# Two attention layers on one core: ones column in layer B's values, the gate folded into the last output weights, activations in two tiles

## The chip, the cores and the metric

The program runs on one core of a Trainium2 chip, with its matrix engine (PE), three elementwise engines (DVE, ACT, POOL) and a queue engine (SP) that issues nearly all transfers. The metric is the device time of one execution in microseconds, the median of several runs.

## What is computed

Two layers over 1024 tokens of width 1024, with 256 context tokens beside them, one batch. Layer A is grouped-query attention with 16 query and 4 key heads, and layer B is neighbourhood attention (a window of 8 rows by 16 columns on a 16 x 64 grid, and all context tokens) with a learned bias. In both, a gate path `silu(z)` multiplies the attention's output ahead of the output projection.

```python
def reference(x, c, ctx, c_ctx, norm_g, w_mod, b_mod, ...):
    for i in range(DEPTH):                      # 0: gqa_axial_mixer, 1: neighbourhood_mixer
        sh_x, sc_x, g_x = jnp.split((silu_c @ w_mod[i] + b_mod[i])[:, None, :], 3, axis=-1)
        hx = rms_norm(x, norm_g[i]) * (1.0 + sc_x) + sh_x
        hc = rms_norm(ctx, norm_g[i]) * (1.0 + sc_c) + sh_c
        ...
        x = x + g_x * yx
    return rms_norm(x, final_norm_g)

# in neighbourhood_mixer, for one row of the grid
s_nb = einsum('bqhd,bqkhd->bhqk', qr, kw) * ATTN_SCALE + bias
s_cx = einsum('bqhd,bshd->bhqs', qr, kc) * ATTN_SCALE
p = softmax(concatenate([s_nb, s_cx], -1))
o = p[..., :n_nb] @ vw + p[..., n_nb:] @ vc
yx = (o * silu(z)) @ w_out
```

## The kernel before

**Numbers.** Every float32 factor is held as a high and a low float16 part, and a product is three matmuls: high x high, high x low, low x high. So each tile is "split" (a cast, then a subtraction), weights are scaled by `WS` = 32, and each weight, activation and probability tile exists twice.

**Stages.** Layer A takes the span up to about 700 us. Then comes its output projection (`a_out`, one call for each 128-token tile and each half of the columns), interleaved with layer B's normalisation: `ln_pair` normalises two token tiles xa, xb (four blocks of 512 values a1, a2, b1, b2), forms the combinations that a Strassen-Winograd product needs, splits them and has the DMA transpose them into `hx`. `hx` holds seven blocks for each pair of token tiles: blocks 0 to 2 come from the "a" transposes (`hrb0a`, `hrb2a`, `hrb4a`, `hrb6a`, L701), blocks 3 to 6 from the "s" transposes (`hrb0s` ... `hrb6s`, L712). The string `"l0 o4 l2 o5 o6 l4 o7 o80 l6 o90"` sets the order of these steps.

Layer B works in eight pairs of heads, u = 0 to 7. `b_load` loads and combines a pair's weights, `b_qk` and `b_vz` project it (`winograd`: seven products, tiles `pwq..` and `pwv..`, and the context's products `pbc`, `pvc`), and `b_att` does its attention: scores into `bsn` and `bsc`, the bias added with a running maximum on DVE (L1613), exponentials on ACT as float16 (`bph`) and float32 (`bpf`) with their sums as a second output (L1631 to L1634), the low part by a subtraction on POOL or DVE (`p_split`: each `BEV`-th call goes to DVE whole, the others to POOL in two halves), a DMA transpose, and the product with the values (L1642, L1644) into `bpv`. `fin` divides by the sums, multiplies by the gate path and hands the result to `o_out`, which splits and transposes it into `ob[u]`.

The final projection is cut into two parts over the eight pairs. `b_part` multiplies pairs 0 to 5 for one token tile and one half of the columns, and `b_out` does pairs 6 and 7 of both halves, then the final norm and the store. Each `b_part` ends with a multiply by the gate row `g1` (DVE, L1751) and an add to the residual tile `acc` (POOL, L1752; DVE for the last tile). `ob` of pairs 0 to 6 goes through DRAM (`ob_d`) and comes back as `obf` in the memory of `hx`.

**Order.** The code records generators with due times: an item `(generator, start, end, total)` of `timeline` spreads its steps over that stretch of "pairs", so `b_att(u)` runs from u to u + 1 beside `b_proj(u + 1)`. The class `Planner` then takes all recorded instructions, simulates the five engines with its own costs, and writes an order for each engine; five rounds of `refine` reorder by due times, and the best is kept. So an edit in one place can change the order everywhere, layer A included.

## Time and profile before

| | |
|---|---|
| median of three runs | 1360.35 us (1357.03 to 1361.37) |
| the profiled execution | 1362.21 us, of which the span of instructions is 1360.3 |
| mean granted PE clock | 0.991 |
| PE matmuls | 1309.5 us busy, 14492 instructions |
| DVE, ACT, POOL busy | 1129.6, 976.2, 909.9 us |
| HBM read, written | 91.03 MB, 15.75 MB |

A matmul's record lasts longer than the time to the next start, since matmuls overlap in the pipeline; what a stream of them costs is read from start to start. The view of stretches gives the busy time of each engine in chosen windows and the granted PE clock. The view of groups gives all instructions of one line, tile and shape with the total and mean. A row `x3` of the timeline is three instructions that follow each other.

### The profile page before, as it was taken

How to read it: one execution, taken by the hardware profiler on the slowest of the kernel's cores; microseconds unless marked ns; L12 is line 12 of the kernel's file. 1: busy time of each engine (PE TensorE's matmuls, PEld its weight loads, DVE VectorE, ACT ScalarE, POOL GpSimd, SP SyncE). 2: the span in 40 equal slices, each digit the busy share in tenths (PEclk: the TensorE clock that was granted, in tenths of full speed). 3: DMA queues.
4: the chain of work that ended last, by engine and by line, in shares of the span. 5: the costliest groups of instructions: out<-in, count | busy, mean ns of one | idle time of the engine just before them, and what ended most of it. 6: DMA issues, size and time to landing. Idle time of an engine off the chain costs nothing.

```text
span 1360.3 us, 37879 instructions
## 1 busy us (share of the span) xinstructions
PE 1309.5 (96%) x14492; PEld 923.2 (68%) x14492; DVE 1129.6 (83%) x2603; ACT 976.2 (72%) x2325; POOL 909.9 (67%) x1251
## 2 busy tenths in 40 slices
PE   8999999999999999999999899999999999999994
PEld 4467777777777777776654357868677686876551
DVE  5898687978898787769448898899999999999668
ACT  4654889888888777788733355897978889787443
POOL 2323778777777767788775566586676778755565
PEclk9999999999999999999999999999999999999997
DMA  9634566787874222245237953587677768679953
GB/s 368 186 114 114 118 125 144 153 153 146 141 142 104 66 77 60 57 118 139 79 109 175 219 109 90 115 151 146 121 142 151 150 130 173 126 165 257 262 113 124
DMA packets 390350, 191.58 MB, mean 141 GB/s; under 512 B 349776, under 2 KB 355088, under 8 KB 390168
## 3 DMA queue, kind: packets, MB, share of 16 engines
q1 hardware_dynamic: 389592, 189.13, 61.6%
q8 instruction: 113, 1.85, 0.6%
q14 instruction: 69, 0.57, 0.1%
q10 hardware_dynamic: 576, 0.03, 0.0%
HBM read 91.03 MB, written 15.75 MB: 78 GB/s over the span
## 4 chain that ended last, share of the span: by engine, by line
PE 49%; DVE 24%; ACT 11%; issue 6%; DMA 5%; POOL 4%; DVEq 0%; POOLq 0%; SPq 0%; ACTq 0%
PE pa L1034 12%; PE pob L1747 5%; PE st L1260 3%; PE st L1261 3%; DVE wb L1435 3%; PE pm L1068 3%; PE poa L1353 2%; PE pv L1137 2%; PE pv L1136 2%; PE pv L1138 2%; DVE bpf L1613 2%; DVE bk L1504 2%; DVE bmx L1620 2%; ACT bpf L1633 1%; ACT bph L1631 1%
## 5 line engine op out<-in xcount | busy, mean ns | idle before, releaser
L1130 POOL TENSOR_TENSOR pl<-pf,ph 128x256 f16<-128x256 f32 x400 | 274.8, 712 | 83.3 <-ACT pf L1247 59.0
L1130 POOL TENSOR_TENSOR bph<-bpf,bph 128x256 f16<-128x256 f32 (+1 forms) x192 | 167.5, 889 | 119.0 <-ACT bpf L1633 98.7
L1034 PE MATMUL pa<-wa,x 128*128 128x256 f16 x1536 | 219.3, 272 | 1.0 <-DVE q L822 1.0
L1245 ACT ACTIVATE ph<-st 128x512 f16<-128x512 f32 x240 | 143.2, 602 | 56.4 <-PE st L1261 55.1
L1560 PEld LDWEIGHTS <-hx 128*128 128x128 f16 x2688 | 156.7, 98 | 11.7 <-issue 4.9
L1034 PEld LDWEIGHTS <-x 128*128 128x128 f16 x1536 | 139.7, 97 | 33.2 <-DVE q L822 1.3
L1247 ACT ACTIVATE pf<-st 128x512 f32<-128x512 f32 x240 | 143.2, 603 | 1.9 <-POOL pl L1130 1.2
L1069 DVE TENSOR_REDUCE mxp<-pm 128x1 f32<-128x512 f32 x192 | 127.5, 683 | 16.2 <-PE pm L1068 15.1
L1137 PE MATMUL pv<-v,ph 128*128 128x64 f16 x960 | 122.5, 195 | 0.0
L1136 PE MATMUL pv<-v,ph 128*128 128x65 f16 x960 | 122.1, 193 | 0.0
L1138 PE MATMUL pv<-v,pl 128*128 128x65 f16 x960 | 121.5, 192 | 0.4 <-POOL pl L1130 0.4
L1512 PEld LDWEIGHTS <-wb 128*128 128x128 f16 x672 | 63.5, 99 | 81.2 <-issue 10.9
L1130 POOL TENSOR_TENSOR qpp<-qpf,qpp 128x256 f16<-128x256 f32 (+1 forms) x158 | 94.2, 621 | 33.8 <-ACT qpf L1203 25.7
L1631 ACT ACTIVATE bph<-bpf,bnx 128x384 f16<-128x384 f32 (+1 forms) x128 | 69.9, 581 | 55.7 <-DVE bnx L1623 35.6
L1136 PEld LDWEIGHTS <-ph 128*128 128x128 f16 x960 | 90.7, 96 | 23.2 <-DVE og L1118 1.7
L1137 PEld LDWEIGHTS <-ph 128*128 128x128 f16 x960 | 90.3, 97 | 14.4 <-issue 0.4
L1138 PEld LDWEIGHTS <-pl 128*128 128x128 f16 x960 | 91.1, 99 | 9.4 <-POOL pl L1130 1.1
L1260 PE MATMUL st<-q,k 128*128 128x512 f16 x240 | 90.9, 379 | 1.9 <-ACT pf L1247 1.2
L1261 PE MATMUL st<-q,k 65*128 65x512 f16 x240 | 91.2, 381 | 0.0
L1353 PE MATMUL poa<-woa,oa 128*128 128x512 f16 x384 | 89.7, 379 | 0.0
L1747 PE MATMUL pob<-wob,obf 128*128 128x512 f16 x336 | 79.9, 379 | 0.2 <-DVE tmb L1751 0.2
L1633 ACT ACTIVATE bpf<-bpf,bnx 128x384 f32<-128x384 f32 (+1 forms) x128 | 74.4, 581 | 0.2
(486 smaller groups left out, 4045.6 us busy)
## 6 DMA issues: line engine op xcount, KB each, us to landing
wg<-in_w_mb SPq DMA_DIRECT2D x32, 512.0 KB
wsb<-in_b_wp SPq DMA_DIRECT2D x64, 256.0 KB
wm<-in_w_m SPq DMA_DIRECT2D x16, 512.0 KB
wsa<-in_a_wq SPq DMA_DIRECT2D x32, 256.0 KB
xstage<-in_x SPq DMA_DIRECT2D x8, 512.0 KB
wsoa<-in_a_w_out SPq DMA_DIRECT2D x16, 256.0 KB
x<-in_x SPq DMA_DIRECT2D x8, 512.0 KB
x_d<-x SPq DMA_DIRECT2D x8, 512.0 KB
```

Source lines behind the costliest of these rows:

```text
L1034: T.matmul(ps[:, :, i, :], hA(a, kt, t), wt[w][:, kt, :], start=n == 0, stop=n == 3 * KT - 1)
L1069: V.tensor_reduce(mxs[i][:, t, ch:ch + 1], pm, axis=AX.X, op=ALU.max)
L1130: G.tensor_tensor(lo[:, c], p32[:, c], hi[:, c], op=ALU.subtract)
L1136: T.matmul(pv[:, t, :], hi[:, c], v[:, 0:65], start=first and t == 0, stop=False)
L1137: T.matmul(pv[:, t, 0:HD], hi[:, c], v[:, 65:129], start=False, stop=False)
L1138: T.matmul(pv[:, t, :], lo[:, c], v[:, 0:65], start=False, stop=last and t == n - 1)
L1245: S.activation(ph, st, AF.Exp)
L1247: S.activation(p32, st, AF.Exp)
L1260: T.matmul(so, k1[:, g, kc], q1[:, :, i, :], start=True, stop=False)
L1261: T.matmul(so, k2[0:65, g, kc], q2[0:65, :, i, :], start=False, stop=True)
L1560: T.matmul(ps[:, t * P:(t + 1) * P], hx[a][:, t, blk, kt], wt[j][:, s_, w, kt], start=first and t == 0 and m == 0, stop=last and t == 3 an ...
L1747: T.matmul(ps, ob[kt][:, t, a], wout["b"][hf][b][:, kt, :], start=n == 0, stop=n == 3 * len(kts) - 1)
```

## The change

- **Values.** The value tile gets a column that holds 2 WS^2 (`v1_` is 130 wide: 64 high, the column, 64 low). The product with the probabilities becomes three matmuls of 65, 64 and 65 columns, as in layer A, and the sum of the probabilities arises in PSUM. The sums on ACT, their reduction, and the old `fin` go; `o_evict`, layer A's, takes its place. `BEV` becomes 8.
- **Gate.** `load_wout` multiplies the last output weights by the gate row (POOL) before the split. `b_part` ends with one add on DVE.
- **Activations.** `hx` becomes two tiles for each float16 part, one for blocks 0 to 2 and one for blocks 3 to 6. The final projection's `obf` (two tiles of three pairs) and `acc` (two of four token tiles) take their memory. Pair 6 is no longer stored and reloaded.
- **Residuals** are loaded by halves where `b_part` begins. Final norm: the first half is scaled on ACT and multiplied on POOL, except for the last tile.
- **Smaller ones.** `ln_pair` exchanges DVE and POOL in its combinations, and `a_out` adds tile 7 on DVE. `b_load` does its combinations in three POOL operations, one of them 256 wide. The second copy of q is made by ACT from the source. `b_att(7)` is due by 7.6, the weights from 6.6, `b_out` from 7.61.

```diff
-BEV, BLAG = 4, 4
+BEV, BLAG = 8, 4
...
-            DM.dma_start_transpose(d[:, t, 0:3].rearrange("p a k q -> p (a k) q"),
+            DM.dma_start_transpose(d[0][:, t].rearrange("p a k q -> p (a k) q"),
                                    s_[:, 0:3].rearrange("p a c -> p (a c)"))
         yield 900
-        G.tensor_tensor(b2, b1, b2, op=ALU.add)
-        V.tensor_tensor(b1, a1, b1, op=ALU.subtract)
-        G.tensor_tensor(a1, b2, a1, op=ALU.subtract)
+        V.scalar_tensor_tensor(b2, b1, -1.0, b2, op0=ALU.mult, op1=ALU.subtract)
+        G.tensor_tensor(b1, a1, b1, op=ALU.subtract)
+        V.scalar_tensor_tensor(a1, b2, -1.0, a1, op0=ALU.mult, op1=ALU.subtract)
         V.tensor_tensor(a2, a2, a1, op=ALU.subtract)
...
+                gw = bl.tile([P, 512], F32, name=f"gw{hf}", tag="gw", bufs=1)
+                DM.dma_start(gw, gate[:, hf * 512:(hf + 1) * 512].broadcast_to([P, 512]))
...
+                        G.tensor_tensor(st, st, gw, op=ALU.mult)
...
-            G.tensor_tensor(x1[:, hc], x1[:, hc], tm, op=ALU.add)
+            (V if t == NX - 1 else G).tensor_tensor(x1[:, hc], x1[:, hc], tm, op=ALU.add)
...
-    hx = [bpool.tile([P, 4, 7, 4, P], F16, name=f"hx{p}", tag=f"H{p}") for p in range(2)]
+    hx = [[bpool.tile([P, 4, 3 + j, 4, P], F16, name=f"hx{p}{j}", tag=f"H{p}{j}") for j in range(2)] for p in range(2)]
...
-            G.tensor_tensor(t1, b12, b11, op=ALU.subtract)
-            G.tensor_tensor(t2, b22, t1, op=ALU.subtract)
-            G.tensor_tensor(t3, b22, b12, op=ALU.subtract)
+            G.tensor_tensor(tt[:, 0:2], st[:, 1:3], b12.unsqueeze(1).broadcast_to([P, 2, P]), op=ALU.subtract)
+            G.tensor_tensor(t2, b22, t1, op=ALU.add)
...
-        v1_ = bq.tile([P, NT, 2, P], F16, name=f"bv1{u}", tag="v1")
+        v1_ = bq.tile([P, NT, 2, 130], F16, name=f"bv1{u}", tag="v1")
+        G.memset(v1_[:, :, :, HD:HD + 1], 2.0 * WS * WS)
...
-                    V.tensor_copy(ov[0][oth, i, ts], ov[0][own, i, ts])
+                    S.activation(ov[0][oth, i, ts], src, AF.Copy, scale=sc)
...
-                        S.activation(pf[:, 0:n], pf[:, 0:n], AF.Exp, bias=m, accum_out=sums[:, t % 4, 0:1])
-                        S.activation(pf[:, n:n + 2], cx_, AF.Exp, bias=m, accum_out=sums[:, t % 4, 1:2])
+                        S.activation(pf[:, 0:n], pf[:, 0:n], AF.Exp, bias=m)
+                        S.activation(pf[:, n:n + 2], cx_, AF.Exp, bias=m)
...
-                                T.matmul(pv[:, t % 4, :], pht[:, x_], v1_[:, kt, i, :], start=t % 4 == 0 and x_ == 0,
-                                         stop=False)
-                                T.matmul(pv[:, t % 4, 0:HD], plt[:, x_], v1_[:, kt, i, 0:HD], start=False,
+                                T.matmul(pv[:, t % 4, 0:65], pht[:, x_], v1_[:, kt, i, 0:65],
+                                         start=t % 4 == 0 and x_ == 0, stop=False)
+                                T.matmul(pv[:, t % 4, 0:HD], pht[:, x_], v1_[:, kt, i, 65:129], start=False, stop=False)
+                                T.matmul(pv[:, t % 4, 0:65], plt[:, x_], v1_[:, kt, i, 0:65], start=False,
                                          stop=t % 4 == 3 and x_ == len(keys) - 1)
...
+                    o_evict(bl, pv, og, 4, sz, hf * 4, i, f"b{u}{i}{hf}")
...
-        items.append((b_att(u), u, u + 1, C_BA))
+        items.append((b_att(u), u, u + (1 if u + 1 < NPAIR else 0.6), C_BA))
...
-        obf = bpool.tile([P, NPAIR - 1, NX, 2, P], F16, name="obf", tag="H0")
+            obf = bpool.tile([P, 3, NX, 2, P], F16, name=f"obf{p}", tag=f"H{p}0")
...
+        if not kts[0]:
+            DM.dma_start(fin_c["acc"][t][:, hcs], x1_d[t * P:(t + 1) * P, hcs])
...
-        tm = bq.tile([P, 512], F32, name=f"tmb{t}{hf}{kts[0]}", tag="cc")
-        V.tensor_tensor(tm, ps, fin_c["g1"][:, hcs], op=ALU.mult)
-        eng.tensor_tensor(fin_c["acc"][t][:, hcs], fin_c["acc"][t][:, hcs], tm, op=ALU.add)
+        V.tensor_tensor(fin_c["acc"][t][:, hcs], ps, fin_c["acc"][t][:, hcs], op=ALU.add)
...
+            if hf or t == NX - 1:
+                V.scalar_tensor_tensor(x2[:, hcs], x2[:, hcs], rs[:, 0:1], fg[:, hcs], op0=ALU.mult, op1=ALU.mult)
+            else:
+                S.activation(x2[:, hcs], x2[:, hcs], AF.Copy, scale=rs[:, 0:1])
+                G.tensor_tensor(x2[:, hcs], x2[:, hcs], fg[:, hcs], op=ALU.mult)
```

What the planner made of it is shown at two places; line numbers of the change differ by a few from those of before.

First, DVE at the end of layer B's normalisation, of before. `x16` and `x17` are token tiles 6 and 7, `L677` and `L678` normalise them, `L690` writes the low part that the transposes `hrb6a` and `hrb6s` take, and `L705`, `L707` form combinations:

```order
L658 TENSOR_SCALAR ms_ln_14266<-lssb6b_14264 128x1
L677 SCALAR_TENSOR_TENSOR x16_14056<-x16_14056,rs_ln_14258,lrow10_13846 128x512
L690 TENSOR_TENSOR hrb4s1_14150<-x14_13892,hrb4s0_14149 128x512
L678 TENSOR_TENSOR x16_14056<-x16_14056,lrow00_13844 128x512
L677 SCALAR_TENSOR_TENSOR x17_14161<-x17_14161,rs_ln_14268,lrow10_13846 128x512 x2
L678 TENSOR_TENSOR x17_14161<-x17_14161,lrow00_13844 128x512 x2
L677 SCALAR_TENSOR_TENSOR x16_14056<-x16_14056,rs_ln_14258,lrow10_13846 128x512
L690 TENSOR_TENSOR hrb6a1_14253<-x17_14161,hrb6a0_14252 128x512
L678 TENSOR_TENSOR x16_14056<-x16_14056,lrow00_13844 128x512
L690 TENSOR_TENSOR hrb6a1_14253<-x16_14056,hrb6a0_14252 128x512
L705 TENSOR_TENSOR x17_14161<-x16_14056,x17_14161 128x512
L690 TENSOR_TENSOR hrb6a1_14253<-x16_14056,hrb6a0_14252 128x512
```

The same place in the change, up to the last split of `hrb6s`:

```order
L690 TENSOR_TENSOR hrb6a1_14255<-x16_14058,hrb6a0_14254 128x512
L690 TENSOR_TENSOR hrb6a1_14255<-x17_14163,hrb6a0_14254 128x512
L690 TENSOR_TENSOR hrb6a1_14255<-x16_14058,hrb6a0_14254 128x512
L704 SCALAR_TENSOR_TENSOR x17_14163<-x17_14163 128x512
L1366 TENSOR_TENSOR tm80_14251<-poa80_14226,gt8_14222 128x512
L1443 SCALAR_TENSOR_TENSOR wb000_14358<-wsb000_14360,wb000_14358 128x3x128
L706 SCALAR_TENSOR_TENSOR x16_14058<-x17_14163,x16_14058 128x512
L690 TENSOR_TENSOR hrb6s1_14289<-x17_14163,hrb6s0_14288 128x512
L707 TENSOR_TENSOR x16_14058<-x16_14058 128x512
L690 TENSOR_TENSOR hrb6s1_14289<-x17_14163,hrb6s0_14288 128x512
L690 TENSOR_TENSOR hrb6s1_14289<-x16_14058,hrb6s0_14288 128x512 x2
```

The three splits of `hrb6a` stand together, and the combination between them (`L705`, which took POOL's `L704`) has left for POOL; `L704` and `L706` came from POOL to DVE.

The queue SP at that place, of before (`lrow` are the context's scale and shift rows, `wsb` a weight tile):

```order
L712 DMA_TRANSPOSE hx1_13800<-hrb4s1_14150 128x16x128
L671 DMA lrow11_14448<-mod_d_100 128x1024
L671 DMA lrow01_14446<-mod_d_100 128x1024
L701 DMA_TRANSPOSE hx0_13799<-hrb6a0_14252 128x12x128
L701 DMA_TRANSPOSE hx1_13800<-hrb6a1_14253 128x12x128
L1426 DMA wsb010_14643<-in_b_wp 128x512
L712 DMA_TRANSPOSE hx0_13799<-hrb6s0_14286 128x16x128
```

And of the change:

```order
L712 DMA_TRANSPOSE hx11_13802<-hrb4s1_14152 128x16x128
L701 DMA_TRANSPOSE hx00_13799<-hrb6a0_14254 128x12x128
L701 DMA_TRANSPOSE hx10_13801<-hrb6a1_14255 128x12x128
L1435 DMA wsb010_14642<-in_b_wp 128x512
L671 DMA lrow11_14447<-mod_d_100 128x1024
L671 DMA lrow01_14445<-mod_d_100 128x1024
L712 DMA_TRANSPOSE hx01_13800<-hrb6s0_14288 128x16x128
```

The two `lrow` loads moved from ahead of the `hrb6a` transposes to behind them.

Second, POOL at the end of the program, of before (`acc` with `tmb` is the residual add of a half tile, `rs_fin` the power of the final norm):

```order
L1752 TENSOR_TENSOR acc_23352<-acc_23352,tmb506_24463 128x512
L1752 TENSOR_TENSOR acc_23352<-acc_23352,tmb516_24475 128x512
L660 TENSOR_TENSOR rs_fin_24343<-ms_fin_24341,mhalf_75 128x1
L660 TENSOR_TENSOR rs_fin_24378<-ms_fin_24376,mhalf_75 128x1
L1752 TENSOR_TENSOR acc_23352<-acc_23352,tmb606_24498 128x512
L1752 TENSOR_TENSOR acc_23352<-acc_23352,tmb616_24510 128x512
L660 TENSOR_TENSOR rs_fin_24413<-ms_fin_24411,mhalf_75 128x1
```

And of the change (`fg` is the final norm's weight row):

```order
L660 TENSOR_TENSOR rs_fin_24796<-ms_fin_24794,mhalf_75 128x1
L1763 TENSOR_TENSOR acc1_23715<-acc1_23715,fg_23716 128x512
L660 TENSOR_TENSOR rs_fin_24828<-ms_fin_24826,mhalf_75 128x1
L660 TENSOR_TENSOR rs_fin_24860<-ms_fin_24858,mhalf_75 128x1
L1763 TENSOR_TENSOR acc1_23715<-acc1_23715,fg_23716 128x512 x2
L660 TENSOR_TENSOR rs_fin_24892<-ms_fin_24890,mhalf_75 128x1
```

The residual adds have left POOL. The multiplies by `fg` of tiles 4 to 6 stand among the powers, and two of them ahead of the last power, which is tile 7's.

87 lines of the change are left out of this document (38 added, 49 removed).

## The prediction

> **What bounds the kernel now.** I read the busy table first, then the stretches by stage, then the waits, and only then single instructions.
>
> ```profile
> PE 1309.5 (96%) x14492; PEld 923.2 (68%) x14492; DVE 1129.6 (83%) x2603; ACT 976.2 (72%) x2325; POOL 909.9 (67%) x1251
> ```
>
> TensorE is busy for 96% of the span of 1360.3 us. Whatever is to be won lies in the other 51 us, and whatever adds matmuls is paid in full. Where those 51 us lie is told by the view of stretches (columns: stretch, its length, then busy time and instructions of PE, PEld, DVE, ACT and POOL, then the granted PE clock, the DMA share and GB/s).
>
> ```profile
> 102.00:748.00 646.00, 637.63 (x7689) 462.21 (x7687) 499.12 (x1212) 488.28 (x1061) 470.49 (x677) 1.00 0.53 117
> 748.00:816.00 68.00, 61.17 (x387) 32.17 (x386) 63.04 (x91) 30.79 (x57) 42.27 (x49) 0.92 0.74 165
> 816.00:1326.00 510.00, 498.98 (x5723) 369.66 (x5721) 458.06 (x1043) 391.29 (x1067) 348.54 (x470) 1.00 0.73 153
> 1326.00:1361.00 35.00, 16.14 (x75) 6.94 (x72) 28.36 (x51) 10.71 (x29) 20.31 (x20) 0.77 0.32 120
> ```
>
> PE is idle for 8.4 us in layer A, which the diff hardly touches. It is idle for 6.8 us in the change of layers (748 to 816), where its clock also falls to 0.92 on average, a further loss of 68 x 0.08 = 5.4 us. Eight pairs of layer B leave 11.0 us idle, and the end, to 1360.3, leaves 18.2 us; what is missing from 51 lies in the first 102 us. The change works on the last three stretches shown.
>
> **The end.** The timeline gives the last matmuls and the chain behind them.
>
> ```profile
> 1341.91 0.81 PE L1747 MATMUL pob<-wob,ob 128*128 128x512 f16 x3
> ```
> ```profile
> 1350.35 0.68 DVE L1752 TENSOR_TENSOR acc<-acc,tmb 128x512 f32<-128x512 f32 x1
> 1350.45 0.63 ACT L1760 ACTIVATE jk<-acc 128x512 f32<-128x512 f32 x1 [1.53 <-DVE ms_fin L658]
> ```
> ```profile
> 1354.12 0.15 DVE L1761 TENSOR_TENSOR fss<-fss,fss 128x1 f32<-128x1 f32 x1
> 1354.31 0.15 DVE L658 TENSOR_SCALAR ms_fin<-fss 128x1 f32<-128x1 f32 x1
> 1354.61 0.55 POOL L660 TENSOR_TENSOR rs_fin<-ms_fin,mhalf 128x1 f32<-128x1 f32 x1 [2.66 <-DVE ms_fin L658]
> 1355.19 1.42 DVE L1765 SCALAR_TENSOR_TENSOR acc<-acc,rs_fin,fg 128x512 f32<-128x512 f32 x2 [0.73 <-POOL rs_fin L660]
> ```
>
> The last matmul ends at 1342.7 and the span at 1360.3: 17.6 us without matmuls. They go to a backlog of multiply (DVE), add (POOL) and normalise (DVE) for each half tile; the last residual add starts only 7.6 us after the last matmul. With the gate in the weights, an eviction is one add. My new chain: 0.2 from PE to DVE, the add 0.68, the square 0.63 and its read 0.19, the two small DVE steps 0.30, the power 0.55, two normalises 1.42, some 0.7 for the links, and from their end (1356.6) to the span's end 3.7 as now: 8.4 us. The POOL rows of the change put tile 6's multiply ahead of the last power, and that multiply waits for ACT's scaling of tile 6, which stands behind the last square. I add 1.6 for it (ACT's scaling and one POOL operation of 1.4, the row L1752 below, less the DVE steps that they overlap): 10.0. Gain 7.6; 0.6 us of PE gaps since 1326 (16.7 less 16.1 busy) could go too, but for each tile DVE will have about 2.5 us of work (two adds, a normalise and small steps) beside 2.6 us of matmuls (12, at 0.22 from start to start), and a normalise that meets POOL lasts longer. I take **-7**, with bounds -9 and -4.
>
> **The third matmul.** For every key block and query tile the change turns two matmuls (128 and 64 columns) into three (65, 64, 65). Layer A has this form already, so both are in the trace.
>
> ```profile
> L1642 PE MATMUL bpv<-bv,bpht 128*128 128x128 f16 x608 | 68.7, 220 | 1.1 <-DMA bpht<-bph 1.0
> ```
> ```profile
> 900.78 0.22 PE L1642 MATMUL bpv<-bv,bpht 128*128 128x128 f16 x1
> ...
> 901.12 0.38 PE L1512 MATMUL pwq2b<-hx,wb 128*128 128x512 f16 x1
> ```
> ```profile
> 560.99 0.19 PE L1136 MATMUL pv<-v,ph 128*128 128x65 f16 x1
> 561.01 0.20 PE L1137 MATMUL pv<-v,ph 128*128 128x64 f16 x1
> ...
> 561.42 0.38 PE L1261 MATMUL st<-q,k 65*128 65x512 f16 x1
> ```
>
> Durations overlap, so only starts count. From 900.78 to 901.12 stand four key blocks in the old form: 85 ns each. From 560.99 to 561.42 stand 14 matmuls of the new form: 31 ns each, 92 ns for three. 608 x 7 ns = **+4.3**, bounds +3 and +6, all on the path.
>
> The Trainium skill, "TensorE: Matmul & The Clock Gate", section "Back-to-back issue gap", speaks against this edit: a real stream of weight load and matmul is said to sustain about 81 ns per matmul at 128 columns. By that rule 608 more would cost 49 us; the starts above, 31 ns apart, disagree with it.
>
> **Relief of the helpers in layer B.** The waits of PE in 816 to 1326 are short and mostly for DVE. The longest:
>
> ```profile
> PE pwv7c L1560 <- DVE bv L1542: 1.3, 1, 1.3
> ```
>
> DVE is 90% busy there (458 of 510). What the change takes from it and from ACT, by the groups:
>
> ```profile
> L1659 DVE TENSOR_TENSOR boc<-boc,bse 128x256 f32<-128x256 f32 x32 | 18.2, 570 | 0.1
> L1654 DVE TENSOR_SCALAR bse<-bse 128x4 f32<-128x4 f32 x32 | 13.4, 420 | 0.1
> L1658 DVE TENSOR_TENSOR boc<-bpv,boc 128x256 f32<-128x256 f32 x32 | 13.3, 415 | 1.3 <-ACT boc L1657 1.2
> L1501 DVE COPY bq<-bq 64x512 f16<-64x512 f16 x32 | 17.0, 542 | 0.7
> L1127 DVE TENSOR_TENSOR bph<-bpf,bph 128x640 f16<-128x640 f32 x16 | 16.1, 1006 | 0.5 <-ACT bpf L1634 0.3
> L1634 ACT ACTIVATION_READ_ACCUMULATOR bpf<-bsc,bnx 128x1 f32 x128 | 25.8, 201 | 0.0
> ```
>
> ```profile
> L1116 DVE TENSOR_TENSOR pv<-pv,ors x40: 280/422/433, 159.7 to 698.3; 128x256 f32<-128x256 f32 x24, 128x128 f32<-128x128 f32 x16
> ```
>
> The new eviction is that of layer A: a reciprocal and two multiplies like L1116, at 0.42 us against the 0.57 of L1659. So the add L1658 and the scaling L1654 go (13.3 + 13.4), a small reduction of some 5 too, and two multiplies are cheaper by 0.15 us, 32 times: about 41 us. The copy goes to ACT (17), and half of the 32 splits go to POOL (16). DVE loses some 74 of 458 us. ACT loses these 128 accumulator reads and the 128 of L1633, about 51, and gains 32 copies of 0.6 = 19. POOL gets 16 splits (two halves near 0.9 each, +29) and the gate multiplies of 16 weight tiles, and loses its adds in the final projection and one of four operations of each weight tile:
>
> ```profile
> L1752 POOL TENSOR_TENSOR acc<-acc,tmb 128x512 f32<-128x512 f32 x30 | 41.1, 1379 | 20.6 <-DVE tmb L1751 7.9 <-DMA acc<-x_d 5.0 <-DVE wob L731 4.4
> L1431 POOL TENSOR_TENSOR wtb<-wsb 128x128 f32<-128x128 f32 x64 | 39.6, 619 | 0.0
> ```
>
> So +29 + 22 + 10 (the final norm's multiplies) - 41 - 32 = -12. None of this is on the path by itself; its worth is bounded by the 11.0 us of idle. A single wait comes from the order meeting a late DVE, so I take half, **-5**, with bounds -9 and +4 (a new order has waits of its own; the ACT copy now sits ahead of the scores of the next pair, and POOL's splits get later).
>
> **The change of layers.** PE ends its out-projection at 774.7 and then waits for the transposed activations of the last pair of tiles:
>
> ```profile
> 778.28 0.39 PE L1512 MATMUL pwq0a<-hx,wb 128*128 128x512 f16 x1 [3.62 <-DMA hx<-hrb6a]
> ```
> ```profile
> 770.34 1.52 SPq L671 DMA_DIRECT2D lrow<-mod_d  x2
> 772.63 5.02 SPq L701 DMA_TRANSPOSE hx<-hrb6a  x2
> ```
> ```profile
> 778.37 5.37 SPq L712 DMA_TRANSPOSE hx<-hrb6s  x2
> ```
> ```profile
> 780.00:785.00 5.00, 4.43 (x11) 1.43 (x10) 5.00 (x8) 1.01 (x3) 3.96 (x5) 0.50 1.10 221
> ```
>
> The clock is 0.50 behind the gap. What comes before is DVE's:
> ```profile
> 754.80 0.68 DVE L1357 TENSOR_TENSOR tm<-poa,gt 128x512 f32<-128x512 f32 x1
> ```
> ```profile
> 773.89 0.68 DVE L690 TENSOR_TENSOR hrb6a<-x,hrb6a 128x512 f16<-128x512 f32 x1
> ```
> From that multiply (tile 7's second half) to that last split the order of before has 22 operations, which took 19.8 us, 0.9 each, with waits for POOL's subtraction and ends stretched beside POOL. The change has 21 and two more ahead of them (tile 7's adds and a subtraction, now DVE's), and its one wait for POOL has other work around it. At 0.75 us each they take 17.3, about 2.5 us less. The two lrow loads (1 MB, about 4.9 us of the queue at 221 GB/s) move behind the transposes. But the next blocks come with hrb6s, whose two transposes take 5.4 us of SP; DVE has their last split after nine more operations, so I see them only 2 to 3 us earlier. So PE starts sooner, does 17 matmuls instead of 13 ahead of that (4 x 0.2), and waits there instead: **-3.5**, bounds 0 and -10. What is late next is hrb6s.
>
> The Trainium skill, "TensorE: Matmul & The Clock Gate", section "What's actually happening", says that the clock halves after an idle window of about 3.4 us; the gap of 3.6 and the 0.50 behind it agree. By that rule two shorter waits would keep the full clock, and this term would be about -7, the forecast 1347.
>
> **The loads of the final projection.** The old code loads pairs 0 to 5 in halves of 256 KB, the new one whole.
>
> ```profile
> 1236.52 0.64 SPq L1729 DMA_DIRECT2D obf<-ob_d  x1
> ```
> ```profile
> 1247.77 0.57 SPq L1729 DMA_DIRECT2D obf<-ob_d  x1
> ```
>
> The first six halves (1.5 MB) took from 1236.5 to 1248.3 to issue, among other transfers. PE now needs 3 MB at the same point. Their tile of low blocks comes free earlier by the last product of pair 7 (48 matmuls at 56 ns and what stands between them, some 4 us), the gate row (512 KB) is gone and pair 6 stays on the chip. I put **+1.5** for it, bounds 0 and +17.
>
> **The sum.** -7 + 4.3 - 5 - 3.5 + 1.5 = -9.7. The profiled execution took 1362.2 (span 1360.3 and 1.9 around it), so it would be 1352.5. That execution is 1.9 above the median of 1360.35; against the median the forecast is **1350.7**. The order of layer A is also drawn anew, which I hold to be worth 3 us either way, out of its 8.4 us idle.
>
> **The rivals.**
> 1. Only the end shrinks: -7 + 4.3 gives 1357.6, within 0.3% (4.1 us, about what a measurement can tell from no change). For it: each wait in layer B is under 1.4 us, so slack on DVE need not remove it. Chance 0.16.
> 2. The whole loads come late. If 3 MB go at the rate of those 1.5 MB, the sixth lands 12 us later than now; less the 4 us earlier start, PE idles for 8 and loses about 5 to the half clock, as at 780, and the attention of pair 7 waits behind the loads on SP for some 4. +17 in place of +1.5: 1366, slower. It decides when the six loads take longer than the 19 us (an estimate from the rows between the last reader of the lower tile and the sixth matrix, at 56 ns per 128 columns) that PE has other work. Against it: no wait for obf is listed now. Chance 0.08.
> 3. Each added matmul pays its own weight load:
> ```profile
> L1137 PEld LDWEIGHTS <-ph 128*128 128x128 f16 x960 | 90.3, 97 | 14.4 <-issue 0.4
> ```
> 608 x 97 ns is 59 in place of 4.3: 1405. The starts of layer A are against it. This is the Trainium skill's rule above, at this row's price. Chance 0.03.
> 4. The gaps go wholly: -9 + 4.3 - 9 - 10 gives 1336.7. Chance 0.05.
>
> **How the numbers follow.** The forecast has 0.68. Faster is it and the fourth, 0.73; same is the first, 0.16; slower the second and third, 0.11. The range from 1339 to 1361 takes in most of the forecast's bounds and the first rival; it leaves out the second, the third and the fourth.
>
> **What would show it.** Right: the last matmul within 11 us of the span's end; triples of the third form at about 92 ns; DVE near 75% busy in layer B with under 8 us of PE idle; the first pwq0a before 777 with the next wait on hrb6s. Wrong: a wait of PE on obf, a 0.50 clock after 1230, or new waits on ACT or POOL in layer B that make up for those on DVE.

## The result, and the profile after

The changed kernel takes 1347.24 us in the median (1346.48 to 1347.82, 4 runs) against 1359.9 for the kernel before beside it: a ratio of 0.9906, 95% interval 0.9894 to 0.9918. On another occasion it gave 0.9903 (0.9888 to 0.9918). By the first ratio that is 12.8 us of the 1360.35; the forecast was 1350.7, 3.5 us higher, and the result lies inside its range. The profiled execution has a span of 1346.1 us, 14.2 less than the profiled execution before.

The busy table of the page, then the view of stretches with the columns explained above:

```profile
PE 1309.7 (97%) x15100; PEld 928.7 (69%) x15100; DVE 1072.1 (80%) x2456; ACT 968.4 (72%) x2076; POOL 890.7 (66%) x1214
```
```profile
102.00:748.00 646.00, 639.98 (x7712) 464.81 (x7711) 506.63 (x1221) 490.22 (x1063) 469.15 (x672) 1.00 0.54 118
748.00:816.00 68.00, 62.43 (x514) 37.95 (x513) 62.43 (x94) 35.54 (x65) 41.41 (x49) 1.00 0.73 168
816.00:1326.00 510.00, 502.05 (x6228) 369.88 (x6226) 408.19 (x912) 379.56 (x817) 343.29 (x449) 1.00 0.74 152
1326.00:1361.00 35.00, 9.16 (x42) 3.90 (x40) 13.67 (x23) 8.17 (x20) 8.46 (x9) 0.86 0.20 76
```

PE has 608 more matmuls and the same busy time. From 748 to 816 it is busy for 1.3 us more than before, but does 514 matmuls instead of 387. The granted clock is 1.00 there now, not 0.92, and the program is further along, so that some of the 514 are narrower ones. From 816 to 1326 its idle time fell from 11.0 to 7.95 us, and DVE's busy time from 458 to 408. These windows are fixed while the program became shorter, so part of what lay behind 1326 now lies ahead of it.

The waits of PE, the longest sums of the whole span:

```profile
PE bpv L1650 <- DMA bpht<-bph: 4.1, 6, 1.2
PE pwq0b L1521 <- DVE w1q L1465: 2.2, 1, 2.2
...
PE bsc L1602 <- ACT bpf L1642: 1.5, 2, 1.3
```

The wait of 3.6 us for `hx` is gone, and no wait for `obf` is listed. The one for the transposed probabilities `bpht` has grown from 1.0 to 4.1 us in all. What the queue SP waited for ahead of issuing these transposes points to the low parts that POOL writes (waiting line, released by, us in total, times, longest; before, then changed):

```profile
SPq L1637 <- POOL bph L1130: 51.0, 29, 5.8
```
```profile
SPq L1645 <- POOL bph L1131: 140.1, 58, 5.5
```

The three kernels below with `BEV` = 4 (before, b_ln, b_ln_ord) have a PE wait for `bpht` of 1.0 to 1.2 us, and all others, with `BEV` = 8 and so more of these splits on POOL, 2.2 to 4.3. No run changes `BEV` alone.

**By stage.** For all kernels below I cut the span at the same matmuls: the start of the last `poa` (end of layer A), the first `pwv1c` (end of the change of layers), the last `pwv7c` (layer B), the last `pob` (final projection), and the span's end (tail). These are starts in the traces, in microseconds; the ratio is the recorded one, with its interval. It departs from the quotient of the medians by up to 0.0011 (u_gate), which is 1.5 us.

| kernel | layer A ends | change of layers | layer B | final projection | tail | span | ratio to before |
|---|---|---|---|---|---|---|---|
| before | 774.3 | 97.7 | 363.5 | 106.8 | 18.0 | 1360.3 | 1 |
| changed, first | 772.2 | 90.6 | 362.9 | 109.6 | 10.7 | 1346.1 | 0.9906 (0.9894 to 0.9918) |
| changed, second (after2) | 772.7 | 90.5 | 364.2 | 109.2 | 10.7 | 1347.4 | 0.9903 (0.9888 to 0.9918) |
| u_gate | 773.2 | 90.8 | 361.5 | 111.0 | 15.6 | 1352.1 | 0.9933 (0.9908 to 0.9958) |
| u_pv | 775.0 | 91.7 | 365.8 | 110.6 | 10.6 | 1353.8 | 0.9944 (0.9918 to 0.9969) |
| u_ln | 780.9 | 94.8 | 362.1 | 107.5 | 10.1 | 1355.4 | 0.9969 (0.9941 to 0.9996) |
| u_obf | 773.5 | 91.3 | 361.7 | 105.9 | 10.5 | 1342.8 | 0.9893 (0.9878 to 0.9908) |
| c_plan | 775.4 | 91.1 | 362.4 | 108.1 | 10.9 | 1347.9 | 0.9931 (0.9905 to 0.9957) |
| x_mm4 | 772.8 | 91.9 | 375.2 | 112.8 | 10.7 | 1363.5 | 1.0041 (1.0024 to 1.0058) |
| t6_dve | 773.0 | 91.0 | 362.6 | 109.0 | 10.6 | 1346.1 | 0.9902 (0.9878 to 0.9927) |
| b_ln | 773.9 | 92.2 | 370.0 | 106.8 | 18.4 | 1361.3 | 1.0024 (1.0011 to 1.0037) |
| b_ln_ord | 774.4 | 91.9 | 365.2 | 107.3 | 18.2 | 1356.9 | 0.9978 (0.9968 to 0.9988) |
| b_pv | 780.4 | 100.0 | 364.1 | 107.5 | 18.0 | 1370.0 | 1.0069 (1.0054 to 1.0084) |
| b_ln_pv | 774.2 | 92.6 | 363.8 | 109.0 | 18.5 | 1358.2 | 0.9990 (0.9981 to 0.9999) |

So the 14.2 us between the two spans are -2.1 in layer A, -7.1 in the change of layers, -0.6 in layer B, +2.8 in the final projection and -7.3 in the tail. The two rows of the changed kernel tell how far one profile can be trusted: the same program differs by 1.3 us in layer B and by 0.5 us at most elsewhere. Layer A varies more than that pair shows. PE's order in it is the same, matmul for matmul, in the changed kernel, u_gate, u_pv, u_obf, x_mm4, t6_dve and b_ln_ord, and its end lies anywhere from 772.2 to 775.0, so that the -2.1 is no clear gain. One of the ten executions of b_ln_ord took 2416.88 us at a mean granted clock of 0.72, and its ratio leaves that one out.

### The profile page after: what moved, and what is told of

The parts are those of the page before. It is cut to its first block, busy times and chain, and to the rows that moved or that the text cites. A ratio compares the mean times of both kernels' runs of the same rounds, so it can differ in the third digit from the quotient of the medians.

```text
span 1346.1 us, 38648 instructions
## 1 busy us (share of the span) xinstructions
PE 1309.7 (97%) x15100; PEld 928.7 (69%) x15100; DVE 1072.1 (80%) x2456; ACT 968.4 (72%) x2076; POOL 890.7 (66%) x1214
## 5 line engine op out<-in xcount | busy, mean ns | idle before, releaser
L1131 POOL TENSOR_TENSOR bph<-bpf,bph 128x256 f16<-128x256 f32 (+1 forms) x224 | 184.0, 848 | 89.1 <-ACT bpf L1641 67.7
L1139 PEld LDWEIGHTS <-pl 128*128 128x128 f16 x960 | 91.1, 99 | 9.3 <-POOL pl L1131 0.9
L1438 POOL TENSOR_TENSOR wtb<-wsb 128x256 f32<-128x256 f32 x64 | 56.3, 881 | 32.5 <-DMA wsb<-in_b_wp 11.0
```

Source lines behind the costliest of these rows:

```text
L1131: G.tensor_tensor(lo[:, c], p32[:, c], hi[:, c], op=ALU.subtract)
L1139: T.matmul(pv[:, t, :], lo[:, c], v[:, 0:65], start=False, stop=last and t == n - 1)
```

## The experiments

Kernels whose name begins with u_ are the changed kernel with one part undone, those with b_ the kernel before with parts of the change.

**The gate undone (u_gate).** The gate row is multiplied in at the end again, and the add goes to POOL, except for the last part of the last tile. The weights are no longer multiplied by it.

```diff
-    items.append((load_wout(b_w_out, "b", gate_d[1, 0:1, :]), 6.6, 7.2, 1600))
+    items.append((load_wout(b_w_out, "b"), 6.6, 7.2, 1600))
...
-        V.tensor_tensor(fin_c["acc"][t][:, hcs], ps, fin_c["acc"][t][:, hcs], op=ALU.add)
+        tm = bq.tile([P, 512], F32, name=f"tmb{t}{hf}{kts[0]}", tag="cc")
+        V.tensor_tensor(tm, ps, fin_c["g1"][:, hcs], op=ALU.mult)
+        (V if t == NX - 1 and kts[0] else G).tensor_tensor(fin_c["acc"][t][:, hcs], fin_c["acc"][t][:, hcs], tm, op=ALU.add)
```

> The changed kernel with the gate taken back out of the weights: each part of the final projection ends again with a multiply by the gate row (DVE) and an add to the residual (POOL, DVE for the last tile); the due times, the halves of the residual loads and all else stay changed. Theory (the double eviction makes the backlog of the end): from the last matmul to the end about 16 us against 10.3, so +5 to +8 us, 1352 to 1355. Rival (the earlier due times of pair 7 and of the last tiles made the end short, the eviction does not matter): the end stays under 12 us and the time within 2 us of 1347.

Measured: 1353.09 us, ratio 0.9933. The tail is 15.6 us for 10.7. DVE's and POOL's timelines show the backlog back: the residual add of a half tile takes DVE or POOL's time after its multiply, and the last three normalisations stand at the very end.

```profile
1339.17 1.12 DVE L1750 TENSOR_TENSOR acc<-acc,tmb 128x512 f32<-128x512 f32 x1
1340.39 0.69 DVE L1749 TENSOR_TENSOR tmb<-pob,g 128x512 f32<-128x512 f32 x1
1341.12 0.84 DVE L1750 TENSOR_TENSOR acc<-acc,tmb 128x512 f32<-128x512 f32 x1
...
1345.00 3.08 DVE L1764 SCALAR_TENSOR_TENSOR acc<-acc,rs_fin,fg 128x512 f32<-128x512 f32 x3
```
```profile
1339.70 1.71 POOL L1750 TENSOR_TENSOR acc<-acc,tmb 128x512 f32<-128x512 f32 x1
```

The gate's place is worth 4.9 of the 7.3 us of the tail. It is the tail that shows it (10.1 to 10.9 us in every other kernel with the folded gate); the whole time doesn't, since another order alone gives nearly the same one (c_plan). The other 2.4 go with what stays in this kernel: loads by halves, ACT and POOL in the final norm, new due times. They were not taken apart.

**The old normalisation (u_ln).** `ln_pair`'s combinations as in the kernel before (this changes the sign of some blocks that the projections read, and so the result; the work stays the same) and tile 7's add on POOL.

```diff
-        V.scalar_tensor_tensor(b2, b1, -1.0, b2, op0=ALU.mult, op1=ALU.subtract)
-        G.tensor_tensor(b1, a1, b1, op=ALU.subtract)
-        V.scalar_tensor_tensor(a1, b2, -1.0, a1, op0=ALU.mult, op1=ALU.subtract)
+        G.tensor_tensor(b2, b1, b2, op=ALU.add)
+        V.tensor_tensor(b1, a1, b1, op=ALU.subtract)
+        G.tensor_tensor(a1, b2, a1, op=ALU.subtract)
...
-            (V if t == NX - 1 else G).tensor_tensor(x1[:, hc], x1[:, hc], tm, op=ALU.add)
+            G.tensor_tensor(x1[:, hc], x1[:, hc], tm, op=ALU.add)
```

> The changed kernel with the old combinations in layer B's normalisation (POOL, DVE, POOL, DVE) and tile 7's residual add back on POOL. Theory (DVE waited for POOL and ran stretched beside it, so the hrb6a split ended late): the last hrb6a split comes 6 to 8 us later after the multiply of tile 7's second half, PE waits 3 to 5 us for hx again with the 0.50 clock behind, +4 to +7 us. Rival (the two lrow loads ahead of the transposes were the delay): with lrow still behind the transposes, PE waits under 1 us for hx and the time is within 2 us of 1347.

Measured: 1357.34 us, ratio 0.9969, which by the ratios is 8.6 us more than the changed kernel. But 8.7 us of the span lie ahead of the end of layer A, where nothing was edited: the planner had drawn another order. With the matmuls of layer A so late, the wait for `hx` hardly shows (0.6 us, where the theory had 3 to 5), and the last split of `hrb6a` comes 15.0 us after the multiply of tile 7's second half, 3.1 later than in the changed kernel and not 6 to 8. Only 4.2 us lie in the change of layers. The run says less of the normalisation than of the order, and the edit had to be tried from the other side (b_ln).

**The old product with the values (u_pv).** Two matmuls of 128 and 64 columns, sums on ACT, the old eviction.

```diff
-                                T.matmul(pv[:, t % 4, 0:65], pht[:, x_], v1_[:, kt, i, 0:65],
-                                         start=t % 4 == 0 and x_ == 0, stop=False)
-                                T.matmul(pv[:, t % 4, 0:HD], pht[:, x_], v1_[:, kt, i, 65:129], start=False, stop=False)
-                                T.matmul(pv[:, t % 4, 0:65], plt[:, x_], v1_[:, kt, i, 0:65], start=False,
+                                T.matmul(pv[:, t % 4, :], pht[:, x_], v1_[:, kt, i, :], start=t % 4 == 0 and x_ == 0,
+                                         stop=False)
+                                T.matmul(pv[:, t % 4, 0:HD], plt[:, x_], v1_[:, kt, i, 0:HD], start=False,
...
```

> The changed kernel with the old two matmuls per key block, the sums on ACT and the old eviction (its intermediate kept in the place of the result, since the memory for its own tile is taken). Theory (the third matmul costs PE 4.3 us and the relief of DVE and ACT gives about as much back): -2 to +2 us, PE's start-to-start time per key block from 92 to 85 ns, DVE busier by 40 us in layer B and its waits longer. Rival A (relief is worth nothing): -4.3 us, 1343. Rival B (each added matmul pays a weight load): -50 us.

Measured: 1354.2 us, ratio 0.9944, which by the ratios is 5.2 us more than the changed kernel; the theory allowed 2, and 2.8 of the profile's 7.7 us lie in layer A, in the same order of its matmuls. Fewer matmuls, and yet layer B and the final projection take 3 to 4 us more (476.4 for 472.5 and 473.4). The stretch row goes with that: PE is idle for 15.1 us (7.95 and 9.65 in the changed kernel's two profiles), DVE is busy for 33 us more than in the changed kernel and ACT for 33 too. The run speaks against the rival that relief is worth nothing, but 3 to 4 us are not much more than an order alone moves, as the next run shows.

```profile
816.00:1326.00 510.00, 494.88 (x5660) 366.19 (x5658) 440.92 (x1005) 412.14 (x1104) 354.20 (x445) 1.00 0.75 152
```

**Another order (c_plan).** Only a number of the planner's last search differs.

```diff
-        plan.refine(5, 100.0, 300.0)
+        plan.refine(5, 100.0, 320.0)
```

> The changed kernel with one number of the planner changed (margin of the due times 320 in place of 300), so that the same work is ordered anew on every engine. It is the control for what a new order alone moves. Theory: within 2 us of 1347. Rival (much of the 12.7 us is a lucky order): more than 4 us slower.

Measured: 1352.2 us, ratio 0.9931, though its profiled span is 1347.9. The profiled execution is the fastest of ten. By the medians the kernel is 5.0 us slower than the changed one, by the ratios 3.4: the theory's 2 us did not hold, and the rival, a share of luck in the order of the changed kernel, is nearer. By stage layer A ends 2.7 to 3.2 us later, which is little more than what it varies by in one order, and the rest is 1 to 2 us shorter in sum. So differences of some 3 us in a stage, or 5 in a whole time, mean little between the runs here.

**A fourth matmul (x_mm4)**, with the changed kernel itself (after2), the new normalisation alone (b_ln) and tile 6's final product (t6_dve) on the same chip. Layer A's order is that of the changed kernel.

```diff
+                                T.matmul(pv[:, t % 4, 0:HD], plt[:, x_], v1_[:, kt, i, 65:129], start=False, stop=False)
                                 T.matmul(pv[:, t % 4, 0:65], plt[:, x_], v1_[:, kt, i, 0:65], start=False,
```

> The changed kernel once more, timed on the same chip as the three kernels beside it, so that each of them is measured against it. All theories: about 0.990 of the kernel before (0.989 to 0.992), with the span by stage within 1 us of the first profile: last matmul of layer A at 772, 91 us to the first block of values, 363 us of layer B, 110 us of the end with the last matmul, tail 10.7 us.

> The changed kernel with one more 64-column matmul per block of keys (the low part of the probabilities by the low part of the values), 608 in all, the rest and layer A's order as they are. It is the price of an added matmul by itself. Theory (an added matmul on the same weights costs about its columns' time, 31 ns as between the starts in the profile): +18.8 us on the changed kernel, all of it in layer B and the end. Rival 1 (each added matmul waits for its own weight load): +49 us at 81 ns, or +34 us at the 56 ns that 128-column matmuls with a load each took. Rival 2 (the PE is not the bound in these stretches, so an added matmul falls into its waits): under +8 us.

Measured: 1348.38 us for the changed kernel, as expected but for layer B (364.2 for 363), and 1365.54 with the added matmuls, 17.2 us for 608: 28 ns each, in layer B (+11.0 on after2), the final projection (+3.6) and, with 1.4, the change of layers. That is near the theory's 31 ns. The Trainium skill ("TensorE: Matmul & The Clock Gate", "Back-to-back issue gap") gives 81 ns for a weight load and a matmul of 128 columns, which would have been 49 us. No run here shows that figure: matmuls of 128 columns with a weight load each start every 56 ns in this kernel (the median of 2568 neighbours in the products `pwv`), and the added ones have 64 columns. In the page's row PE has 608 matmuls more and is busy for 16.8 us more than in the changed kernel's first profile: they were paid in full.

```profile
PE 1326.5 (97%) x15708; PEld 945.9 (69%) x15708; DVE 1068.0 (78%) x2456; ACT 968.8 (71%) x2076; POOL 890.8 (65%) x1214
```

**Tile 6's final product on DVE (t6_dve).**

```diff
-            if hf or t == NX - 1:
+            if hf or t >= NX - 2:
```

> The changed kernel with the final normalisation of tile 6's first half on VectorE (one operation) instead of ScalarE and GpSimd. In the changed kernel's tail VectorE's 0.74 us product takes 1.75 us and its 0.16 us addition 1.21 us while GpSimd multiplies 512 columns beside them. Theory (VectorE is held up by GpSimd's operations there): the tail falls from 10.7 to 9.3 us, 1.3 us faster, too little for the timing and read from the profile. Rival (those durations are only how the records show a wait for ScalarE): VectorE gets 0.7 us more to do, and the tail grows by 0.7 us.

Measured: 1348.87 us, a tail of 10.6. Neither came. DVE's timeline, the changed kernel first, then this one:

```profile
1336.71 1.75 DVE L1760 SCALAR_TENSOR_TENSOR acc<-acc,rs_fin,fg 128x512 f32<-128x512 f32 x1
1338.38 1.21 DVE L1755 TENSOR_TENSOR fss<-fss,fss 128x1 f32<-128x1 f32 x1
```
```profile
1336.93 2.41 DVE L1760 SCALAR_TENSOR_TENSOR acc<-acc,rs_fin,fg 128x512 f32<-128x512 f32 x2
1339.26 0.15 DVE L1755 TENSOR_TENSOR fss<-fss,fss 128x1 f32<-128x1 f32 x1
```

The small addition takes 0.15 us again when no POOL multiply of 512 columns lies beside it, so that stretch was POOL's doing. Another one in the changed kernel agrees: it ends when POOL's multiply does, at 1333.65 and 1333.63.

```profile
1332.42 1.23 DVE L1755 TENSOR_TENSOR fss<-fss,fss 128x1 f32<-128x1 f32 x1
```
```profile
1332.14 1.49 POOL L1763 TENSOR_TENSOR acc<-acc,fg 128x512 f32<-128x512 f32 x1 [0.83 <-ACT acc L1762]
```

But the two products ahead of it (0.74 each where POOL is quiet) take 2.41 together, beside the POOL multiply that is left, and the gain is used up.

**The normalisation alone (b_ln), and in another order (b_ln_ord).** The lines of u_ln's diff the other way round, put into the kernel before.

> The kernel before with two things of the change alone: the combinations of the layer normalisation in their new form (two on VectorE instead of GpSimd, the subtraction on GpSimd) and tile 7's last addition on VectorE. The order of layer A's matmuls is then that of the kernel before to the last one, which the undoing of these lines in the changed kernel didn't keep. It changes the sign of some of the blocks that the projections read. Theory (VectorE's and GpSimd's waits for each other at the change of layers are the whole of that gain): the stretch from the last matmul of layer A to the first block of values falls from 97.7 to 91 or 92 us, all else stays, 6 to 7 us faster than before (ratio 0.995 to 0.996). Rival 1 (the forecast's term): the transposes of the second half come due next, 3.5 us faster (0.9974). Rival 2 (the stretch is shorter because of the new halves of the activation tile or the fewer weight operations of the change): no change, 0.998 to 1.001.

Measured: 1364.43 us, ratio 1.0024. The change of layers is 92.2 us, close to the theory's 91 to 92 and not the forecast's 3.5 less. But the whole is slower and not 6 to 7 us faster: layer B takes 6.5 us more. DVE, busy for 94% of 774 to 1236 before, is busy for 95%:

```profile
774.00:1236.00 462.00, 445.21 (x5349) 340.94 (x5347) 435.31 (x968) 363.55 (x966) 322.78 (x456) 0.99 0.70 140
```
```profile
774.00:1236.00 462.00, 442.65 (x5340) 339.46 (x5338) 439.86 (x965) 362.50 (x964) 325.11 (x455) 1.00 0.68 139
```

(The first row is the kernel before, the second b_ln.) I took this for a second bound: PE can't be earlier while DVE has the same work left. Three runs were to tell this from bad luck with the order.

```diff
-BP0, BP1 = 0, 0.95
+BP0, BP1 = 0, 0.92
```

> The run with the new layer normalisation alone (with its changed signs) in another order: the due time of the projections is 0.92 for 0.95, from which the planner draws another order of the same work in both layers. Read by stage, since layer A's end moves too. Theory (VectorE as second bound): VectorE has the same work, so layer B stays at 367 us or more with the change of layers at 91 to 93. Rival (bad luck of the order): layer B 361 to 365.

Measured: 1357.96 us, ratio 0.9978: layer B 365.2. The same work in another order lost 1.7 us in layer B, not 6.5. DVE is busy for 441 of the 462 us here too. It is nearer to the rival: some 5 of the 6.5 us were the order.

**The product with the values alone (b_pv), and with the normalisation (b_ln_pv).** The edits of u_pv's diff, reversed, with the short eviction and `BEV` = 8.

> The kernel before with one other part of the change alone: the column of ones, the three matmuls per block of keys, the short eviction, and the splits of the probabilities as in the change (8 for 4). Layer normalisation, gate, loads and weights stay old. What is asked is why the new layer normalisation alone gained 5.5 us at the change of layers (97.7 to 92.2) and lost 6.5 us in layer B (363.5 to 370.0). Theory (VectorE, busy 94 to 95% from 774 to 1236 us, is a second bound of layer B: PE cannot come earlier as long as VectorE has the same work left): relief of VectorE without an earlier start gives layer B a little, 360 to 363 us by stage for 363.5, the end 1 us more (99 of the added matmuls at 28 us per 1000), change of layers unchanged at 97 to 98; in all 0 to 3 us faster, ratio 0.998 to 1.000. Rival (relief and order have nothing to do with each other, each added matmul simply costs): layer B 365 to 368, ratio 1.002 to 1.004.

Measured: 1369.54 us, ratio 1.0069, which nobody expected. Layer B is 364.1 us, the same as before, where the theory had 360 to 363 and the rival 365 to 368. The loss lies in layer A (6.1 us later, order) and in the change of layers: PE waits twice for the first pair's weights on DVE, and behind both waits its clock is at one half, for 3.4 and 6.8 us (the waits from 745 to 875 us; then the stretch from 800 us, behind the second).

```profile
PE pwq0b L1513 <- DVE wb L1435: 4.1, 1, 4.1
PE pwq0a L1513 <- DVE wb L1435: 4.1, 1, 4.1
```
```profile
800.00:805.00 5.00, 4.03 (x14) 1.83 (x15) 4.46 (x8) 2.89 (x6) 2.18 (x4) 0.50 0.56 114
```

> The kernel before with both parts, the new layer normalisation (with the sign of some of the blocks that the projections read changed) and the new probabilities by values with its short eviction. Layer A's matmuls stand as in the kernel before and as in the run with the new layer normalisation alone. Theory (VectorE as second bound): with VectorE relieved the earlier start is kept: change of layers 91 to 92.5 us, layer B 361 to 364, in all 5 to 8 us faster than before, ratio 0.994 to 0.9965, which is more than the two alone together (+3.5 and about -1 us). Rival (the loss in layer B with the new layer normalisation alone was the order that the planner happened to draw, or the start itself): layer B 366 to 370 again, in all 0 to 4 us slower, ratio 1.000 to 1.003.

Measured: 1359.44 us, ratio 0.9990. The change of layers stays short (92.6), layer B is 363.8, and the final projection takes 2.2 us more. Layer B is as the theory has it; the total isn't, by 4 us.

What follows from the four: the new normalisation takes 5.1 to 5.8 us out of the change of layers in each of the three kernels that have it. Layer B gives back between 0.3 and 6.5 of them. For DVE's load as the reason speaks b_ln_pv, 6.2 us shorter in layer B than b_ln; but it is only 1.4 us shorter than b_ln_ord, and those two, with the same work, differ by 4.8. DVE as a second bound isn't shown.

**The loads by halves (u_obf).**

```diff
-        for p in range(2):
-            obf = bpool.tile([P, 3, NX, 2, P], F16, name=f"obf{p}", tag=f"H{p}0")
-            for j in range(3):
-                DM.dma_start(obf[:, j].rearrange("p t a q -> p (t a q)"), ob_d[3 * p + j])
-                ob[3 * p + j] = obf[:, j]
+        obfs = [bpool.tile([P, 3, NX, 2, P], F16, name=f"obf{p}", tag=f"H{p}0") for p in range(2)]
+        for t in (0, 4):
+            for u in range(6):
+                DM.dma_start(obfs[u // 3][:, u % 3, t:t + 4].rearrange("p t a q -> p (t a q)"),
+                             ob_d[u, :, t * 2 * P:(t + 4) * 2 * P])
+                ob[u] = obfs[u // 3][:, u % 3]
```

> The changed kernel with the outputs of pairs 0 to 5 loaded back in halves of four query tiles, all first halves first, as the kernel before did, instead of whole pairs. The forecast put 1.5 us on the whole loads, with 17 us as the far end; the stretch from the last block of values to the last matmul was 109 to 110 us against 106.8 before. Theory (no matmul of the last projection waits for a load, and the 2.5 us are the 99 added matmuls and order): nothing, 0.990 to 0.992, that stretch 108.5 to 110. Rival (the whole loads of 512 KB lie ahead of the last transposes of probabilities on SP's queue and make them late): that stretch 106 to 107.5 and the waits of the matmuls for those transposes under 1.5 us in all instead of 3.4 to 4.1.

Measured: 1345.46 us, ratio 0.9893, the fastest kernel here. The final projection takes 105.9 us for 109.2 and 109.6, less than the rival's 106 to 107.5. The same stretch in the changed kernel, its second profile and here:

```profile
1235.00:1245.00 10.00, 7.95 (x73) 4.49 (x71) 3.64 (x7) 5.42 (x12) 5.17 (x7) 0.88 1.09 270
```
```profile
1235.00:1245.00 10.00, 7.29 (x89) 4.92 (x88) 3.05 (x9) 6.77 (x17) 4.99 (x7) 1.00 1.08 235
```
```profile
1235.00:1245.00 10.00, 10.00 (x100) 5.97 (x98) 6.76 (x20) 6.78 (x17) 8.15 (x12) 1.00 0.98 206
```

PE is idle for 2 to 3 us there in the changed kernel and not at all here. What SP issued from 1215 to 1260 tells what stood ahead of the transposes (columns: name, queue, kind and count, KB each, median us to landing; the changed kernel, then u_obf):

```profile
acc<-x_d SPq DMA_DIRECT2D x14, 256.0 KB, 4.3
obf<-ob_d SPq DMA_DIRECT2D x6, 512.0 KB
...
bpht<-bph SPq DMA_TRANSPOSE x11, 3.6
```
```profile
obf<-ob_d SPq DMA_DIRECT2D x12, 256.0 KB, 4.0
acc<-x_d SPq DMA_DIRECT2D x5, 256.0 KB
...
bpht<-bph SPq DMA_TRANSPOSE x14, 3.5
```

14 transposes instead of 11 were issued in the same time. The rival has the stage right, but not the sign by which it was to be read: the waits for `bpht` in the whole span fell only to 3.0 us. They could hardly have fallen more, since 3.5 of the 4.1 us lie ahead of the final projection. Whether the smaller loads did it or the order that came with them (five residual loads for 14) is open. Order alone moves this stage by 2 us: u_ln and c_plan keep the whole loads and take 107.5 and 108.1. PE's idle time in it is 2.6 to 5.1 us in the eight profiles with whole loads and 1.3 to 3.6 in the six with halves, which points to the loads but doesn't separate them. Against the changed kernel the whole times overlap (0.9878 to 0.9908 and 0.9888 to 0.9918), so that it beats it is seen in that stage alone.

## Why the prediction was right

**The end, -7:** measured -7.3, and -4.9 of it goes when the gate is undone. From the last matmul's end (1335.8) to the span's end are 10.4 us, predicted 10.0. Inside it one step was wrong. The 1.6 us were put on POOL, which was to hold up the last power; but POOL took it 0.15 us after DVE's step had ended. DVE was late instead, by 1.0 us each in the two rows shown with t6_dve.

```profile
1339.63 0.15 DVE L658 TENSOR_SCALAR ms_fin<-fss 128x1 f32<-128x1 f32 x1
```
```profile
1339.93 0.55 POOL L660 TENSOR_TENSOR rs_fin<-ms_fin,mhalf 128x1 f32<-128x1 f32 x1 [0.35 <-DVE ms_fin L658]
```

**The third matmul, +4.3:** right. Summed over all `bpv` matmuls, the time to the next matmul's start went from 53.0 to 58.4 us, +5.4 with the waits in it (59.8 in the second profile), and two neighbours are 31 ns apart in the mean; x_mm4 prices an added one at 28 ns. The third rival is out.

**The helpers, -5:** right in sign, too large. PE's idle time in 816 to 1326 fell by 3.1 us (1.4 in the second profile). Read by stage it fell from 8.4 to 5.2 us in layer B (6.0 in the second profile) and rose from 1.6 to 3.0 (3.8) in the final projection. DVE is 80% busy in the window, not 75, partly because work of the end now falls into it (28.4 us of DVE behind 1326 became 13.7). Counting each moment once, the copy, the splits and the eviction take 65 us less, not 74. The mis-sized part is the eviction, 33 us less instead of 41, since the groups' means count overlapped ends twice. And the longest idle time that is left is no longer DVE's: the wait for the transposes (`bpht`, 4.1 us) took its place. The prediction had it in half a sentence ("POOL's splits get later") and gave it no price; the SP rows above show it.

**The change of layers, -3.5:** too small, measured -7.1, and -5.5 in the kernel before with that edit alone. Two steps failed. First, DVE's operations were taken at 0.75 us each; these rows are the first and the last of the stretch:

```profile
751.98 0.69 DVE L1366 TENSOR_TENSOR tm<-poa,gt 128x512 f32<-128x512 f32 x1 [1.36 <-PE poa L1362]
...
761.98 1.89 DVE L690 TENSOR_TENSOR hrb6a<-x,hrb6a 128x512 f16<-128x512 f32 x3
```

That is 21 instructions in 11.9 us, 0.57 each, without one wait for POOL; the prediction's 17.3 were 23 at 0.75. With this edit alone, in the kernel before, and with the product by values beside it (b_ln, b_ln_ord, b_ln_pv), the same stretch takes 13.0 to 14.3 us. In the old form it took 19.8 in the kernel before and 15.0 and 15.1 in u_ln and b_pv, so that part of the difference is again the order. Second, "What is late next is hrb6s" is wrong. Its transposes came 8.5 us earlier (769.85 for 778.37), not 2 to 3, PE never waited for `hx`, and what came late instead were ACT and DVE with the Winograd combinations:

```profile
769.85 5.71 SPq L712 DMA_TRANSPOSE hx<-hrb6s  x2
```
```profile
772.43 2.75 PE L1521 MATMUL pwq0a<-hx,wb 128*128 128x512 f16 x12
776.15 1.24 PE L1521 MATMUL pwq0a<-hx,wb 128*128 128x512 f16 x5 [0.96 <-ACT e1q L1461]
```

The longest such wait is 2.2 us, and the granted clock stays at 1.00. In this stage PE's idle time fell from 8.3 to 5.9 us, and the 10.2 us at half clock (778.6 to 788.8), worth about 5.1 (an estimate: half of them), went: together about the 7.1.

The Trainium skill's rule ("TensorE: Matmul & The Clock Gate", "What's actually happening"), that the clock halves after an idle window of about 3.4 us, agrees with the traces of before and changed in this stage: 0.50 behind 3.6 us, 1.00 behind 2.2. The prediction had worked out about -7 and 1347 from it and preferred its own term; the rule gave the nearer number. But not every run agrees with it as it was read. In u_obf the same wait, 2.15 us for 2.16, has 3.4 us at half clock behind it (the changed kernel first, then u_obf):

```profile
786.40 0.81 PE L1521 MATMUL pwq0b<-hx,wb 128*128 128x512 f16 x3 [2.16 <-DVE w1q L1465]
...
787.10 2.11 PE L1521 MATMUL pwq0b<-hx,wb 128*128 128x512 f16 x9
```
```profile
787.64 0.85 PE L1521 MATMUL pwq0b<-hx,wb 128*128 128x512 f16 x3 [2.15 <-DVE w1q L1465]
...
788.39 3.74 PE L1521 MATMUL pwq0b<-hx,wb 128*128 128x512 f16 x9
```

Nine matmuls took 2.11 us in one and 3.74 in the other. Of the ten profiles whose longest wait in this stage is 2.0 to 2.7 us, seven keep the full clock there and three (u_obf, u_pv, b_ln_ord) don't. So that the changed kernel lost no clock there was in part luck.

**The loads, +1.5:** not settled. The final projection took 2.4 to 2.8 us more, of which the third matmul explains 0.7 (99 key blocks at 7 ns), and with the loads in halves 0.9 less than before. But b_pv and b_ln_pv, with the old loads and the three matmuls, also take 0.7 and 2.2 us more than before. So the sign is likely and the size open. PE waited for `obf` once, for 1.5 us in the second profile, and in the first no such wait is listed. The "0.50 clock after 1230" came in part: the clock is 0.88 in the mean from 1235 to 1245 in the first profile, 1.00 in the second.

**Layer A, 3 us either way:** too narrow for an order drawn anew. Its end moved by -2.1 us in the changed kernel, which is within what one order varies by, but by +6.1 and +6.6 in b_pv and u_ln, neither of which edits its matmuls.

**Two slips in the working,** neither in the sum: 1 MB at 221 GB/s is 4.7 us and not 4.9, and POOL's three operations for each weight tile save 20 us (156.5 to 136.6), not 32.

So the spans differ by 14.2 us where the sum had 9.7. The change of layers gave 3.6 us more than forecast, and layer A 2.1, which the sum did not hold. Layer B and the final projection together, forecast at 4.3 - 5 + 1.5 = +0.8, came to +2.2 (+3.1 in the second profile). The tail was right in place and size, and the third matmul in its price. That the median came within 3.5 us of the forecast is partly luck: errors of opposite sign, and an order whose redrawing alone moved it by 3.4 to 5.0 us.

## What to carry to other kernels

Read a chain's pace where its engine does not wait for another: 0.57 us per DVE operation, not the mean of a stretch with waits in it. A shortened chain can be worth the clock behind its gap as well. Price a matmul in a stream by start to start, and test it by adding one. When work moves to an engine off the path, ask which transfers start with what that engine writes: the splits moved to POOL are what the transposes, and behind them PE, then waited for. And where one edit redraws the order of a whole program, compare stages between kernels that share the order up to there; here a whole time alone could be off by 5 us and more for reasons that have nothing to do with the edit.

## What was unexpected of the hardware

An operation of 0.15 us on DVE took 1.21 us beside a POOL multiply of 512 columns, and 0.15 once that multiply was gone; a product of 0.74 us took 1.75. And the PE clock was halved for 3.4 us behind a wait of 2.15 us in u_obf, and behind one of 1.33 us in the changed kernel (0.50 from 1242.6 to 1245.9), but not behind one of 2.16 in the changed kernel.
